# Reordering the two row-to-column boundaries of a transformer layer: tile 1's last gated residual behind tile 0's first normalised columns

## The chip, the cores and the metric

The kernel runs on one core of a Trainium2 chip. The metric is the device time of one execution in microseconds (us). The kernel before took 1943.88 us, the median of three runs (1939.19 to 1945.11).

The core has five engines that run their own instruction streams and wait for each other through semaphores: TensorE (PE in the profile, PEld for its weight loads), VectorE (DVE), ScalarE (ACT), GpSimd (POOL) and SyncE (SP, which here only issues DMAs).

## The reference

One layer over 256 tokens with 2048 features, all in float32: a SwiGLU feed-forward block, a token mixer (8 heads of softmax attention with forget gates, 4 heads of mLSTM), and a second SwiGLU block. Each block reads a modulated layernorm of the residual `x` and adds its result back through a gate, and each sum is layernormed again. Cut to what matters:

```python
ada = (silu(c) @ w_ada + b_ada)[:, None, :]
sh1, sc1, g1, sh2, sc2, g2, sh3, sc3, g3 = split(ada, 9, axis=-1)
h = swiglu(layernorm(x) * (1 + sc1) + sh1, ffn1_w_in, ffn1_w_out)
x = layernorm(ALPHA * x + 0.5 * (1 + g1) * h, ln1_g, ln1_b)
h = token_mixer(layernorm(x) * (1 + sc2) + sh2, w_in, ..., w_out)
x = layernorm(ALPHA * x + (1 + g2) * h, ln2_g, ln2_b)
h = swiglu(layernorm(x) * (1 + sc3) + sh3, ffn2_w_in, ffn2_w_out)
x = layernorm(ALPHA * x + 0.5 * (1 + g3) * h, ln3_g, ln3_b)
```

## The kernel before, in words

**Layout.** The residual `res` lies with tokens on partitions: two tiles of 128 tokens (`a` = 0 and 1), 2048 features each. The products read features on partitions: `xT` holds 16 blocks of 128 features by 256 tokens. Every float32 operand of the large products is split into a rounded part (`hi`, a cast on ACT, L142) and a rest (`lo`, a subtraction on DVE, L143), and each product is three matmuls (L367 to L369).

**A boundary.** Between a block's output product and the next block's first product the residual must be finished, normalised twice and turned from rows into columns. The function `boundary` does this, once after the first feed-forward block (the first boundary) and once after the mixer (the second one). Just ahead of it PE runs the held products of the last 512 columns, first all of tile 0, then all of tile 1. The steps, for each tile:

- `add_up`: gate times product (L431), residual (L433), statistics of the last 512 columns (L436). `row_std` then combines the statistics (L257, L259), and POOL takes the reciprocal root `rs` (L247).
- `ln_affine`: the layernorm with its gain and bias (L484, L489). ACT squares the result and sums the squares (L494).
- `ln_stats`: mean and variance of the new rows from these sums (L500 to L513). It pauses at two places: after L509, ahead of L511, which is the first step that reads ACT's sums of squares, and after POOL has been given the reciprocal root `mr` (L247), ahead of L517.
- `modulate_tile`: normalise two blocks of 128 columns (`n`: on DVE, L309, for the very first pair; on ACT, L311, for all others), transpose them on PE (`tp`, L315), scale and shift into `xf` (ACT L325, DVE L322), and split into `xhi` and `xlo` (ACT L331, DVE L332).

The first three loads of the next block's weights (`raw_mo` in the first boundary, `raw_gu` in the second) arrive early, in the three buffers that there are; the products from them (L618, `cols_1024`) read the unsplit `xf` directly, first for all of tile 0, then for all of tile 1. The fourth load waits for the buffer of the first.

**The order.** On DVE the order within a boundary is the order in which the code is written (`manual_schedule`): the function takes single steps from generators with `next`, so that the tiles' chains interleave. All other engines, and DVE elsewhere, are ordered by a scheduler from estimated durations; so a change of DVE's order in the boundary can move instructions on them too. Each engine runs its instructions in that order.

**The modulation stream.** The vector `ada` is computed beside the main products: weights of `w_ada` are streamed in (`ar`), multiplied and added on DVE (`acc`, L155 and L157), split, and summed over partitions by PE (`bc`, L170). `ada_gate` does this for a gate, in two halves of 1024 columns (`j`), each half in two parts of 512 (`i`). The gate's bias row from `b_ada` is loaded straight into `gate` by a DMA that POOL issues (L203), and L210 adds the sums to it. There is one `gate` tile: the load of the next gate's half must wait until the boundary's last L431 on these columns has read the old one. The stream is advanced a few steps at a time by `pump`; a `PAUSE` ends such a turn. `need` runs it until a given part is done.

Of the kernel before, what the change touches and what calls it, by code (L numbers as in the profile page):

```python
# [14 lines left out]
P = 128  # L15
# [17 lines left out]
def layer_kernel(  # L33
# [8 lines left out]
    V, S, G_, PE, SP = nc.vector, nc.scalar, nc.gpsimd, nc.tensor, nc.sync  # L42
# [104 lines left out]
    gate = cst.tile([P, D], F32, name="gate")  # L147
# [5 lines left out]
    def ada_acc(acc, raw, k):  # L153
        if k == 0:
            V.tensor_scalar_mul(acc, raw, csil[:, k:k + 1])  # L155
        else:
            V.scalar_tensor_tensor(out=acc, in0=raw, scalar=csil[:, k:k + 1], in1=acc,  # L157
                                   op0=ALU.mult, op1=ALU.add)


    def ada_split(acc, tag):
        ahi = ap.tile([P, 512], F32R, tag="ahi", name=f"ahi{tag}")
        alo = ap.tile([P, 512], F32R, tag="alo", name=f"alo{tag}")
        split(acc, ahi, alo)
        return ahi, alo

    def ada_sum(parts, tag):
        bc = aux_tile(f"bc{tag}")
        for i in range(2):
            PE.matmul(bc, onesr, parts[i], start=i == 0, stop=i == 1)  # L170
        return bc
# [22 lines left out]
    def ada_gate(v, s):  # L194
        for j in range(2):
            c0 = v * D + j * 1024
            acc = ap.tile([P, 1024], F32, tag="acc", name=f"acc{v}_{j}")
            for k in range(KD):
                raw = ap.tile([P, 1024], F32, tag="araw", bufs=2, name=f"ar{v}_{j}_{k}")
                SP.dma_start(raw, w_ada[0, k * P:(k + 1) * P, c0:c0 + 1024])  # L200
                ada_acc(acc, raw, k)
                yield
            G_.dma_start(gate[:, j * 1024:(j + 1) * 1024], b_ada[0:1, c0:c0 + 1024].to_broadcast([P, 1024]))  # L203
            for i in range(2):
                parts = ada_split(acc[:, i * 512:(i + 1) * 512], f"{v}_{j}_{i}")
                for _ in range(2):
                    yield PAUSE
                bc = ada_sum(parts, f"{v}_{j}_{i}")
                gs = gate[:, j * 1024 + i * 512:j * 1024 + (i + 1) * 512]
                V.scalar_tensor_tensor(out=gs, in0=bc, scalar=1.0, in1=gs, op0=ALU.add, op1=ALU.add)  # L210
                if s != 1.0:
                    V.tensor_scalar_mul(gs, gs, s)

    ada_left = {}
    PAUSE = 1
# [34 lines left out]
    def together(*gens):  # L250
        gens = list(gens)
        while gens:
            gens = [g for g in gens if next(g, 0) is None]


    def row_std(mv, rs, st):
        V.bn_aggr(mv, st)  # L257
        yield
        V.tensor_scalar_add(mv[:, 1:2], mv[:, 1:2], EPS)  # L259
        yield  # L260
        rsqrt(rs, mv[:, 1:2])
        yield

    def small(n, tag, name):
        return (wp if tag == "sums" else sm).tile([P, n], F32, tag=tag, bufs=4, name=name)
# [214 lines left out]
    def ln_affine(a, rs, mv, lgb, sums, tag):  # L480
        for h in range(2):
            cs = slice(h * (D // 2), (h + 1) * (D // 2))
            r = res[:, a, cs]
            V.scalar_tensor_tensor(out=r, in0=r, scalar=mv[:, 0:1], in1=lgb[0][:, cs],  # L484
                                   op0=ALU.subtract, op1=ALU.mult)
            yield
        for i, (c0, c1) in enumerate(((0, 1024), (1024, 1536), (1536, 2048))):
            r = res[:, a, c0:c1]
            V.scalar_tensor_tensor(out=r, in0=r, scalar=rs, in1=lgb[1][:, c0:c1], op0=ALU.mult, op1=ALU.add,  # L489
                                   accum_out=sums[:, i:i + 1])  # L490
            if i == 0:
                V.tensor_scalar_mul(sums[:, 4:5], sums[:, 0:1], -2.0 / D)
            sq = npool.tile([P, 1024], F32, tag="sq", name=f"sq_{tag}{a}{i}")
            S.activation(sq[:, :c1 - c0], r, AF.Square, bias=sums[:, 4:5], accum_out=sums[:, 7 + i:8 + i])  # L494
            yield


    def ln_stats(out_, sums):
        s = [sums[:, i:i + 1] for i in range(10)]
        V.tensor_tensor(out=s[1], in0=s[1], in1=s[2], op=ALU.add)  # L500
        yield
        mean = out_[:, 2:3]
        V.tensor_scalar(out=mean, in0=s[0], scalar1=s[1], scalar2=-1.0 / D, op0=ALU.add, op1=ALU.mult)
        yield
        V.tensor_scalar(out=s[3], in0=s[1], scalar1=s[0], scalar2=1.0 / D, op0=ALU.subtract, op1=ALU.mult)
        yield
        V.tensor_scalar(out=s[2], in0=s[3], scalar1=s[3], scalar2=-1.0, op0=ALU.mult, op1=ALU.mult)
        yield
        V.tensor_scalar_add(s[2], s[2], EPS)  # L509
        yield 1  # L510
        V.tensor_scalar(out=s[6], in0=s[7], scalar1=s[8], scalar2=s[9], op0=ALU.add, op1=ALU.add)  # L511
        yield
        V.tensor_scalar(out=s[6], in0=s[6], scalar1=1.0 / D, scalar2=s[2], op0=ALU.mult, op1=ALU.add)  # L513
        yield
        rsqrt(out_[:, 0:1], s[6])
        yield 1
        V.tensor_tensor(out=out_[:, 1:2], in0=mean, in1=out_[:, 0:1], op=ALU.mult)  # L517
        yield
# [4 lines left out]
    def boundary(add_up, st, lgb, v, tag, xT, entry, nk):  # L523
        mv, rs, sums, mr = ([small(n, t, f"{t}_{tag}{a}") for a in range(2)]
                            for n, t in ((2, "mv"), (1, "rs"), (10, "sums"), (3, "mr")))
        xs = {}
        with tc.manual_schedule(engines={mybir.EngineType.DVE}):
            for _ in add_up(0):
                pass
            together(row_std(mv[0], rs[0], st[0]))  # L530
            aff = [ln_affine(a, rs[a], mv[a], lgb, sums[a], tag) for a in range(2)]
            lns = [ln_stats(mr[a], sums[a]) for a in range(2)]
            for _ in aff[0]:
                pass
            together(lns[0])
            up = add_up(1)
            next(up)
            together(lns[0])
            m = [[modulate_tile(v, a, k, 2, mr[a], xT, xs if k < 6 else None, a + k == 0) for k in range(0, 8, 2)]
                 + [modulate_tile(v, a, k, 2, mr[a], xT) for k in range(8, nk, 2)] for a in range(2)]  # L540
            m0, m1 = m
            next(m0[0])
            together(lns[0])
            next(m0[1])
            next(up)
            next(up, 0)
            together(row_std(mv[1], rs[1], st[1]))
            next(m0[0])
            next(aff[1])
            next(m0[2])  # L550
            next(aff[1])
            next(m0[1])
            next(aff[1])
            next(m0[2])
            next(aff[1])
            next(aff[1])
            together(lns[1])
            next(m0[0])
            next(m0[1])
            together(lns[1])  # L560
            together(lns[1])
            next(m1[0])
            next(m1[1])
            next(m1[0])
            next(m1[2])
            next(m1[1])
            next(m1[2])
            for i in range(3, len(m0)):
                next(m0[i])
                next(m1[i])  # L570
                next(m0[i])
                next(m1[i])
                if i == 3:
                    for b in (m0[2], *m1[:3]):
                        next(b)
                for b in (m0[i], m1[i]):
                    next(entry, None)
                    last = next(b)
        return last, mr, xs
# [52 lines left out]
    def entry_of(load, got, u0, u1):  # L632
        for u in range(u0, u1):
            got[u] = []
            for item in load(u):
                got[u].append(item)
                yield
# [185 lines left out]
    with tc.manual_schedule(engines={mybir.EngineType.DVE, mybir.EngineType.Activation}):  # L823
        next(fa)
    ada_queue(ada_gate(2, 0.5), ada_pair(3, range(4)), ada_pair(6, range(2)), ada_gate(5, 1.0),
              ada_pair(6, range(2, 3)), ada_pair(6, range(3, 4)), ada_gate(8, 0.5))
    for j in range(4):
        fa = first_ada(j + 1) if j < 3 else load_mixer_smalls()
# [71 lines left out]
    raws = [mo_raw(u) for u in range(3)]  # L900
    mow = {}
    fence, _, xs = boundary(*ent["f"], lgb, 3, "1", xT, entry_of(mo_load, mow, 3, 6), KD)
    lnp.release()

# [456 lines left out]
    for j in range(2, 10):  # L1361
# [6 lines left out]
        for f in range(2):  # L1368
            i = 2 * j + f
# [10 lines left out]
    for j in range(2, 10):  # L1380
# [7 lines left out]
        for f in range(2):  # L1388
            i = 2 * j + f
# [51 lines left out]
```

## Time and profile before

| | |
|---|---|
| median of 3 runs | 1943.88 us (1939.19 to 1945.11) |
| the profiled execution | 1942.6 us, span of the trace 1940.9 us |
| mean granted PE clock in it | 0.994 |
| busy: PE, DVE, ACT, POOL | 1899.0, 1473.1, 945.6, 56.4 us |
| DMA | 510.90 MB, mean 263 GB/s |

The span is the time from the first to the last instruction of the profiled execution; its own time is that of the whole execution. In rows of a timeline the columns are the start in us, the duration in us, the engine, the line of the kernel, the operation, output and inputs by the names of the program, the shapes, and in brackets how long the engine stood idle before it and what ended that. In rows of stretches they are the stretch, its length, the busy time of each engine with its number of instructions, the granted PE clock (1.00 is full speed), the busy share of the DMA engines and their GB/s. In rows of a line's instructions the three numbers are the shortest, the median and the longest duration in ns.

### The profile page before, as it was taken

How to read it: one execution, taken by the hardware profiler on the slowest of the kernel's cores; microseconds unless marked ns; L12 is line 12 of the kernel's file. 1: busy time of each engine (PE TensorE's matmuls, PEld its weight loads, DVE VectorE, ACT ScalarE, POOL GpSimd, SP SyncE). 2: the span in 40 equal slices, each digit the busy share in tenths (PEclk: the TensorE clock that was granted, in tenths of full speed). 3: DMA queues.
4: the chain of work that ended last, by engine and by line, in shares of the span. 5: the costliest groups of instructions: out<-in, count | busy, mean ns of one | idle time of the engine just before them, and what ended most of it. 6: DMA issues, size and time to landing. Idle time of an engine off the chain costs nothing.

```text
span 1940.9 us, 32198 instructions
## 1 busy us (share of the span) xinstructions
PE 1899.0 (98%) x13069; PEld 1720.3 (89%) x13069; DVE 1473.1 (76%) x1818; ACT 945.6 (49%) x1336; POOL 56.4 (3%) x82
## 2 busy tenths in 40 slices
PE   6999999999999999999999999999999999999997
PEld 3999999999988888598999785998999999988886
DVE  5879988777788998688887787777766665555776
ACT  3554454443454554735755534655444444444552
POOL 1111100000000000100000000000000000000000
PEclk8999999999999999999999999999999999999999
DMA  9978869999999786499888883987776775655552
GB/s 352 382 263 313 319 229 304 305 314 311 303 321 314 273 297 210 142 312 319 266 304 289 281 295 139 315 303 243 246 255 224 269 239 196 234 185 191 194 195 87
DMA packets 295693, 510.90 MB, mean 263 GB/s; under 512 B 10834, under 2 KB 158706, under 8 KB 294520
## 3 DMA queue, kind: packets, MB, share of 16 engines
q1 hardware_dynamic: 287768, 480.53, 72.7%
q0 software_dynamic: 7776, 28.32, 4.1%
q8 instruction: 102, 1.67, 0.3%
q14 instruction: 47, 0.39, 0.1%
HBM read 506.71 MB, written 2.10 MB: 262 GB/s over the span
## 4 chain that ended last, share of the span: by engine, by line
PE 76%; issue 11%; DMA 6%; DVE 5%; ACT 1%; POOL 0%; SPq 0%; DVEq 0%; ACTq 0%; POOLq 0%
PE gu_f L369 8%; PE gu_f L367 8%; PE gu_f L368 8%; PE o_f L367 7%; PE o_f L369 7%; PE o_f L368 7%; PE s L367 4%; PE s L368 4%; PE s L369 4%; DMA ar<-in_w_ada_dram 3%; PE fh L367 2%; PE fh L369 1%; PE fh L368 1%; PE fs L367 1%; PE fs L369 1%
## 5 line engine op out<-in xcount | busy, mean ns | idle before, releaser
L157 DVE SCALAR_TENSOR_TENSOR acc<-ar,csil,acc 128x1024 f32<-128x1024 f32 x242 | 307.7, 1272 | 87.9 <-DMA ar<-in_w_ada_dram 86.7
L367 PE MATMUL s<-xhi_f,hi_s 128*128 128x256 f32 x768 | 213.2, 278 | 0.0
L368 PE MATMUL s<-xlo_f,hi_s 128*128 128x256 f32 x768 | 213.0, 277 | 0.0
L369 PE MATMUL s<-xhi_f,lo_s 128*128 128x256 f32 x768 | 212.8, 277 | 0.0
L369 PE MATMUL gu_f<-xhi_f,lo_f2i 128*128 128x256 f32 x768 | 212.0, 276 | 0.0
L367 PE MATMUL gu_f<-xhi_f,hi_f2i 128*128 128x256 f32 x768 | 212.0, 276 | 0.0
L368 PE MATMUL gu_f<-xlo_f,hi_f2i 128*128 128x256 f32 x768 | 212.0, 276 | 0.0
L143 DVE TENSOR_TENSOR lo_f2i<-raw_f2i,hi_f2i 128x1024 fp32r<-128x1024 f32 x96 | 117.5, 1224 | 87.6 <-ACT hi_f2i L142 87.5
L369 PE MATMUL gu_f<-xhi_f,lo_f1i 128*128 128x256 f32 x640 | 176.7, 276 | 0.0
L367 PE MATMUL gu_f<-xhi_f,hi_f1i 128*128 128x256 f32 x640 | 176.7, 276 | 0.0
L368 PE MATMUL gu_f<-xlo_f,hi_f1i 128*128 128x256 f32 x640 | 176.7, 276 | 0.0
L142 ACT CAST hi_f2i<-raw_f2i 128x1024 fp32r<-128x1024 f32 x96 | 100.8, 1050 | 135.2 <-PE gu_f L368 124.3
L142 ACT CAST hi_s<-raw_s 128x1024 fp32r<-128x1024 f32 x96 | 100.6, 1052 | 128.5 <-PE s L368 94.4
L368 PEld LDWEIGHTS s<-xlo_f,hi_s 128*128 128x128 f32 x768 | 144.9, 189 | 0.2 <-DVE xlo_f L299 0.2
L369 PEld LDWEIGHTS s<-xhi_f,lo_s 128*128 128x128 f32 x768 | 144.9, 189 | 0.0
L367 PEld LDWEIGHTS s<-xhi_f,hi_s 128*128 128x128 f32 x768 | 144.7, 189 | 0.0
L368 PEld LDWEIGHTS gu_f<-xlo_f,hi_f2i 128*128 128x128 f32 x768 | 144.1, 188 | 0.2
L367 PEld LDWEIGHTS gu_f<-xhi_f,hi_f2i 128*128 128x128 f32 x768 | 144.1, 188 | 0.2
L369 PEld LDWEIGHTS gu_f<-xhi_f,lo_f2i 128*128 128x128 f32 x768 | 144.1, 188 | 0.0
L143 DVE TENSOR_TENSOR lo_f2o<-raw_f2o,hi_f2o 128x1024 fp32r<-128x1024 f32 x88 | 107.7, 1224 | 44.9 <-ACT hi_f2o L142 44.8
L143 DVE TENSOR_TENSOR lo_s<-raw_s,hi_s 128x1024 fp32r<-128x1024 f32 x96 | 115.6, 1221 | 26.8 <-ACT hi_s L142 26.7
L367 PE MATMUL o_f<-hi_f2o,hh 128*128 128x512 f32 x344 | 135.2, 393 | 0.0
(485 smaller groups left out, 5351.8 us busy)
## 6 DMA issues: line engine op xcount, KB each, us to landing
ar<-in_w_ada_dram SPq DMA_DIRECT2D x227, 512.0 KB, 5.3
raw_f2i<-in_ffn_w_in_dram SPq DMA_DIRECT2D x48, 1024.0 KB, 5.1
raw_s<-in_ffn_w_in_dram SPq DMA_DIRECT2D x47, 1024.0 KB, 7.3
raw_f1o<-in_ffn_w_out_dram SPq DMA_DIRECT2D x44, 1024.0 KB, 7.2
raw_f2o<-in_ffn_w_out_dram SPq DMA_DIRECT2D x44, 1024.0 KB, 5.0
raw_f1i<-in_ffn_w_in_dram SPq DMA_DIRECT2D x40, 1024.0 KB, 7.6
ar<-in_w_ada_dram POOLq DMA_DIRECT2D x48, 512.0 KB, 6.7
raw_mxo<-in_w_out_dram SPq DMA_DIRECT2D x16, 1024.0 KB, 6.0
```

Source lines behind the costliest of these rows:

```text
L142: S.copy(hi, src)
L143: return V.tensor_tensor(out=lo, in0=src, in1=hi.bitcast(F32), op=ALU.subtract)
L157: V.scalar_tensor_tensor(out=acc, in0=raw, scalar=csil[:, k:k + 1], in1=acc, op0=ALU.mult, op1=ALU.add)
L367: PE.matmul(o, ah, bh, start=start, stop=False)
L368: PE.matmul(o, ah, bl, start=False, stop=False)
L369: PE.matmul(o, al, bh, start=False, stop=stop)
```

## The change

In `boundary`, the three steps of `add_up(1)` for tile 1's last 512 columns (gate product, residual, statistics) no longer stand at two places inside tile 0's `ln_stats`; they stand together behind the first step of tile 0's second pair of columns (`m0[1]`). In `ada_gate`, the load of the gate's bias row is written one `PAUSE` later, behind the first part's split.

```diff
@@ ada_gate
-            G_.dma_start(gate[:, j * 1024:(j + 1) * 1024], b_ada[0:1, c0:c0 + 1024].to_broadcast([P, 1024]))
             for i in range(2):
                 parts = ada_split(acc[:, i * 512:(i + 1) * 512], f"{v}_{j}_{i}")
-                for _ in range(2):
-                    yield PAUSE
+                yield PAUSE
+                if i == 0:
+                    G_.dma_start(gate[:, j * 1024:(j + 1) * 1024], b_ada[0:1, c0:c0 + 1024].to_broadcast([P, 1024]))
+                yield PAUSE
                 bc = ada_sum(parts, f"{v}_{j}_{i}")
@@ boundary
             together(lns[0])
             up = add_up(1)
-            next(up)
             together(lns[0])
...
             next(m0[0])
             together(lns[0])
             next(m0[1])
-            next(up)
-            next(up, 0)
+            for _ in up:
+                pass
             together(row_std(mv[1], rs[1], st[1]))
```

In the changed kernel the lines from L203 on stand up to four lines lower and those from L208 to the boundary one lower, so L431 of before is L432 there, and L203 is L207.

DVE in the first boundary, before; `sums_8228` and `mr_8230` are tile 0's, `o_f_7703` is tile 1's last product, `st_f_6242` and `mv_8225` tile 1's statistics:

```order
L509 TENSOR_SCALAR sums_8228<-sums_8228 128x1
L431 TENSOR_TENSOR o_f_7703<-o_f_7703,gate 128x512
L511 TENSOR_SCALAR sums_8228<-sums_8228 128x1
L513 TENSOR_SCALAR sums_8228<-sums_8228 128x1
L309 TENSOR_SCALAR n_8263<-res,mr_8230 128x256
L517 TENSOR_TENSOR mr_8230<-mr_8230 128x1
L433 SCALAR_TENSOR_TENSOR res<-res,o_f_7703 128x512
L436 BN_STATS st_f_6242<-res 128x6
```

The same place in the changed kernel:

```order
L510 TENSOR_SCALAR sums_8228<-sums_8228 128x1
L512 TENSOR_SCALAR sums_8228<-sums_8228 128x1
L514 TENSOR_SCALAR sums_8228<-sums_8228 128x1
L310 TENSOR_SCALAR n_8262<-res,mr_8230 128x256
L518 TENSOR_TENSOR mr_8230<-mr_8230 128x1
L432 TENSOR_TENSOR o_f_7703<-o_f_7703,gate 128x512
L434 SCALAR_TENSOR_TENSOR res<-res,o_f_7703 128x512
L437 BN_STATS st_f_6242<-res 128x6
```

Tile 1's gate product moved from ahead of L511 to behind L517 (now L518). The second boundary changes in the same way.

POOL at the same boundary, before, with what each instruction waits for:

```order
L247 TENSOR_TENSOR rs_8226<-mv_8224,mhalf 128x1 [waits DVE_49]
L203 DMA gate<-in_b_ada_dram 128x1024 [waits DMASW1_49,DVE_49]
L247 TENSOR_TENSOR mr_8230<-sums_8228,mhalf 128x1 [waits DVE_49]
L247 TENSOR_TENSOR rs_8227<-mv_8225,mhalf 128x1 [waits DVE_49]
L247 TENSOR_TENSOR mr_8231<-sums_8229,mhalf 128x1 [waits DVE_49]
```

And in the changed kernel:

```order
L248 TENSOR_TENSOR rs_8226<-mv_8224,mhalf 128x1 [waits DVE_49]
L248 TENSOR_TENSOR mr_8230<-sums_8228,mhalf 128x1 [waits DVE_49]
L207 DMA gate<-in_b_ada_dram 128x1024 [waits DMASW1_49,DVE_49]
L248 TENSOR_TENSOR rs_8227<-mv_8225,mhalf 128x1 [waits DVE_49]
L248 TENSOR_TENSOR mr_8231<-sums_8229,mhalf 128x1 [waits DVE_49]
```

The bias row's load moved from ahead of tile 0's `mr` to behind it. The second boundary has the same swap; the other four loads of bias rows keep their places.

PE in the first boundary where tile 0's products end and tile 1's transposes begin, before (`mo_8484` and `mo_8485` are tile 0's, `mo_8486` and `mo_8487` tile 1's; `raw_mo_8218` is the first weight load, `raw_mo_8222` the third; the first `tp` is tile 1's):

```order
L618 MATMUL mo_8484<-raw_mo_8222,xf_8297 128x512
L618 MATMUL mo_8485<-raw_mo_8222,xf_8297 128x512
L315 MATMUL tp_8322<-ident,n_8320 128x128 x2
L618 MATMUL mo_8484<-raw_mo_8222,xf_8297 128x512
L315 MATMUL tp_8327<-ident,n_8325 128x128 x2
L315 MATMUL tp_8335<-ident,n_8333 128x128 x2
L618 MATMUL mo_8485<-raw_mo_8222,xf_8297 128x512
L618 MATMUL mo_8486<-raw_mo_8218,xf_8330 128x512
```

And in the changed kernel:

```order
L618 MATMUL mo_8484<-raw_mo_8222,xf_8297 128x512
L618 MATMUL mo_8485<-raw_mo_8222,xf_8297 128x512
L618 MATMUL mo_8484<-raw_mo_8222,xf_8297 128x512
L618 MATMUL mo_8485<-raw_mo_8222,xf_8297 128x512
L316 MATMUL tp_8322<-ident,n_8320 128x128 x2
L316 MATMUL tp_8327<-ident,n_8325 128x128 x2
L618 MATMUL mo_8486<-raw_mo_8218,xf_8330 128x512
L316 MATMUL tp_8335<-ident,n_8333 128x128 x2
```

Tile 0's last two products moved ahead of tile 1's first transposes. At the second boundary one such product moves. In the mixer the scheduler also puts four steps `acc6_0` of the modulation stream (L157) one place earlier on DVE, each ahead of a split `lo_mv` of the value columns' weights.

## The prediction

> **What bounds the kernel now.** I read the page first, then the busy times in five stretches, then the timeline of each engine around the two boundaries. The page:
>
> ```profile
> span 1940.9 us, 32198 instructions
> PE 1899.0 (98%) x13069; PEld 1720.3 (89%) x13069; DVE 1473.1 (76%) x1818; ACT 945.6 (49%) x1336; POOL 56.4 (3%) x82
> ```
>
> TensorE (PE) is busy 1899.0 of 1940.9 us, so only about 42 us can be won by scheduling, wherever PE stands still. The stretches (length, then busy time of PE, PEld, DVE, ACT and POOL):
>
> ```profile
> 776.00:810.00 34.00, 30.13 (x98) 15.35 (x97) 18.25 (x44) 20.94 (x46) 3.21 (x4) 1.00 0.34 105
> 810.00:1186.00 376.00, 368.86 (x2408) 332.31 (x2407) 313.70 (x460) 202.74 (x354) 6.07 (x9) 1.00 0.86 290
> 1186.00:1217.00 31.00, 27.94 (x79) 13.84 (x79) 16.42 (x44) 18.38 (x42) 3.21 (x4) 0.94 0.24 80
> 1217.00:1930.00 713.00, 711.37 (x5055) 660.95 (x5053) 476.87 (x524) 340.70 (x438) 1.52 (x1) 1.00 0.68 226
> ```
>
> The first boundary (776 to 810) has 3.9 us without PE, the second (1186 to 1217) 3.1 us. Behind the second PE hardly stops (1.6 us in 713), so what is won there reaches the end. The mixer between them leaves 7.1 us idle. PE at the first boundary:
>
> ```profile
> 777.49 0.40 PE L369 MATMUL o_f<-hi_f1o,hl 128*128 128x512 f32 x1
> 780.69 0.41 PE L315 MATMUL tp<-ident,n 128*128 128x128 f32 x2 [2.80 <-DVE mr L517]
> 782.88 7.89 PE L618 MATMUL mo<-raw_mo,xf 128*128 128x512 f32 x18
> 791.24 0.44 PE L315 MATMUL tp<-ident,n 128*128 128x128 f32 x2 [0.46 <-ACT n L311]
> ```
>
> Its last product ends at 777.89; it then waits 2.80 us for tile 0's first normalised columns, and later 0.46 for tile 1's. The rows of VectorE (DVE), ScalarE (ACT) and GpSimd (POOL) say why:
>
> ```profile
> 766.91 0.70 DVE L431 TENSOR_TENSOR o_f<-o_f,gate 128x512 f32<-128x512 f32 x1 [5.72 <-PE o_f L369]
> 769.39 0.15 DVE L259 TENSOR_SCALAR mv<-mv 128x1 f32<-128x1 f32 x1
> ...
> 775.52 0.15 DVE L509 TENSOR_SCALAR sums<-sums 128x1 f32<-128x1 f32 x1
> 777.93 0.70 DVE L431 TENSOR_TENSOR o_f<-o_f,gate 128x512 f32<-128x512 f32 x1 [2.25 <-PE o_f L369]
> 778.53 0.27 DVE L511 TENSOR_SCALAR sums<-sums 128x1 f32<-128x1 f32 x1
> 778.83 0.21 DVE L513 TENSOR_SCALAR sums<-sums 128x1 f32<-128x1 f32 x1
> 780.13 0.41 DVE L309 TENSOR_SCALAR n<-res,mr 128x256 f32<-128x256 f32 x1 [1.08 <-POOL mr L247]
> 780.46 0.15 DVE L517 TENSOR_TENSOR mr<-mr 128x1 f32<-128x1 f32 x1
> ...
> 782.26 0.15 DVE L259 TENSOR_SCALAR mv<-mv 128x1 f32<-128x1 f32 x1
> ```
>
> ```profile
> 776.20 0.18 ACT L494 ACTIVATION_READ_ACCUMULATOR sq<-res,sums 128x1 f32 x1
> ```
>
> ```profile
> 778.93 0.58 POOL L203 DMA_DIRECT2D gate<-in_b_ada_dram  x1 [7.76 <-DVE sums L511]
> 779.52 0.57 POOL L247 TENSOR_TENSOR mr<-sums,mhalf 128x1 f32<-128x1 f32 x1
> ```
>
> ACT has tile 0's sum of squares at 776.38, but L511, which reads it, stands in DVE's order behind L431 of tile 1, and L431 waits for PE's last product. Then the reciprocal root `mr` waits once more: on POOL it stands behind the bias row's load, whose issue ends at 779.51.
>
> **The change at the first boundary.** It takes both things out of the way, and needs both: with L431 behind `mr` but the load, which waits for L431, ahead of it, the two engines would wait for each other.
>
> Tile 0: L511 can start at 776.42. From L511 to L513 is 0.30 as before; L513 takes 0.21, the root 0.57, and two hand-overs 0.04 each (780.09 to 780.13): L309 at 777.58 instead of 780.13, 2.55 us earlier. PE's transposes follow 0.56 behind L309 (780.69 against 780.13), at 778.14: PE's wait shrinks from 2.80 to 0.25.
>
> Tile 1: L431 now follows L517, at 777.58 + 0.33 + 0.07 = 777.98, only 0.05 later than before, since it had waited for PE anyway. But nothing of tile 0 stands inside its chain now. From L431 to the start of L259 is 2.48 us where the chain runs alone (766.91 to 769.39), so L259 comes at 780.46 instead of 782.26: tile 1 is 1.80 us earlier. Its order on all engines down to its first transposes is as before, so those could start at 789.44 instead of 791.24.
>
> PE between: before, it had done ten of tile 0's twelve L618 products by 790.77 (the x18 are nine of them, two records each, so about 0.86 us a product). Now ten end at 788.22, and by the new order on PE the last two come next, to 789.94. Tile 1's transposes are ready by then; PE no longer waits and stands 1.30 us earlier and two products (1.72) further, 3.0 us in all. I take 0.5 off: the two products had covered tile 1's way from transposes to features, which now runs bare (0.46 us for one such ACT step). That leaves **2.5 us**; bounds 1.3 (no use of the earlier products) and 3.0.
>
> Next in line is the fourth weight load, which needs the buffer of the first:
>
> ```profile
> 798.13 14.18 SPq L342 DMA_DIRECT2D raw_mo<-in_w_in_dram  x5
> ```
>
> It is released by PE's own tile 1 products, which move by about the same 2.5 us, so it moves along rather than becoming the bound.
>
> The load that stepped back: it is now issued once L431 ends, at about 778.7, on POOL between the two roots; tile 1's `rs` wants POOL only at 780.46 + 0.15 + 0.04 = 780.65. The issue costs 0.58, so nothing waits. All 48 loads of L746, issued from POOL beside the work of DVE, took about the same:
>
> ```profile
> L746 POOL DMA_DIRECT2D ar<-in_w_ada_dram x48: 707/722/889, 28.1 to 228.4; - x48
> ```
>
> [...]
>
> The bias row's later place otherwise costs nothing: its first reader (L210) comes a whole pause later still, and the other four such loads keep their place among POOL's rows.
>
> **The change at the second boundary.** The rows again:
>
> ```profile
> 1188.79 0.70 DVE L431 TENSOR_TENSOR o_mx<-o_mx,gate 128x512 f32<-128x512 f32 x1 [2.33 <-PE o_mx L369]
> 1190.98 0.41 DVE L309 TENSOR_SCALAR n<-res,mr 128x256 f32<-128x256 f32 x1 [1.07 <-POOL mr L247]
> 1193.12 0.15 DVE L259 TENSOR_SCALAR mv<-mv 128x1 f32<-128x1 f32 x1
> ```
>
> ```profile
> 1188.84 0.19 ACT L494 ACTIVATION_READ_ACCUMULATOR sq<-res,sums 128x1 f32 x1
> 1201.44 1.09 ACT L311 ACTIVATE n<-res,mr 128x256 f32<-128x256 f32 x2 [1.41 <-DVE mr L517]
> ```
>
> ```profile
> 1191.54 0.41 PE L315 MATMUL tp<-ident,n 128*128 128x128 f32 x2 [2.79 <-DVE mr L517]
> 1203.16 0.38 PE L315 MATMUL tp<-ident,n 128*128 128x128 f32 x2
> ```
>
> Here ACT delivers only at 1189.03, later than L431 could start. L511 starts at 1189.06, and L309 1.16 behind it as above, at 1190.22: 0.76 us earlier. L431 starts at 1190.62, and 2.48 later L259 at 1193.10: tile 1 gains nothing. PE's wait falls from 2.79 to 2.03. At 1203.16 PE itself was late for tile 1, because of its clock (stretch, PE busy, granted clock):
>
> ```profile
> 780.00:783.00 3.00, 2.05 (x9) 1.00 0.55 180
> ...
> 1193.00:1196.00 3.00, 3.00 (x6) 0.50 0.01 4
> ```
>
> After a gap of 2.79 us the clock was halved for some 3.4 us, 1.7 us of work; after the 2.80 at the first boundary it was not. If the shorter gap leaves it whole, tile 1's transposes start when ready. At the first boundary they stood 0.66 behind the start of tile 1's n:
>
> ```profile
> 790.58 1.09 ACT L311 ACTIVATE n<-res,mr 128x256 f32<-128x256 f32 x2 [1.41 <-DVE mr L517]
> ```
>
> So here they start at 1201.44 + 0.66 = 1202.10, with one product (0.86) more done: 1.06 + 0.86 - 0.5 for lost cover = 1.4. If the clock is halved again, 0.76. I take **1.3**.
>
> [...]
>
> **The sum:** 2.5 + 1.3 = 3.8 us. The profiled execution took 1942.6 (span 1940.9 and 1.7 around it), so 1938.8 for its like; it lay 1.3 below the median of 1943.88 (1939.19 to 1945.11), so **1940.1** for the median. That is 0.2% and within the 0.3%, 5.8 us, which a measurement of this kernel can about tell from no change. The bounds of the two terms, 1.3 + 0.8 to 3.0 + 1.9 (no cover lost), give 1939.0 to 1941.8.
>
> **The rivals.**
>
> *More than the sum: halved clocks go too.* A gap in the mixer was also followed by a slowed clock:
>
> ```profile
> 955.00:960.00 5.00, 5.00 (x37) 0.79 0.88 306
> ```
>
> In this stretch alone 0.21 of 5 us is lost, 1.0. If the median execution, unlike the profiled one, also has a halved clock at the first boundary, to which a gap of 0.25 gives no occasion, that adds 790.77 + 1.7 - 791.24 = 1.2; if the shifted mixer escapes its own, 1.0 more: 3.8 + 2.2 = 6.0, and, with nothing taken off for cover, 7.1: 1937.9 to 1936.8, I say 1937.4. For it: the profiled run is faster than the median. [...]
>
> *Given back in the mixer.* PE waits there for softmax steps that share DVE with the modulation stream, and that stream waits for its weights:
>
> ```profile
> 1071.00 0.33 PE L1058 MATMUL ptp<-ident,s 128*128 128x128 f32 x1 [2.39 <-ACT s L1053]
> ```
>
> If those weights come no earlier, the first boundary's 2.5 us become a longer wait here, and 1.3 remain: 1942.6. Against: their loads are issued in one queue with the products' own, so all move together.
>
> *POOL is slow.* The same root has two durations there:
>
> ```profile
> L247 POOL TENSOR_TENSOR rs<-mv,mhalf x4: 1514/1522/1534, 769.6 to 1193.4; 128x1 f32<-128x1 f32 x4
> L247 POOL TENSOR_TENSOR mr<-sums,mhalf x4: 548/561/572, 779.5 to 1200.7; 128x1 f32<-128x1 f32 x4
> ```
>
> If `mr` now takes 1.52 instead of 0.56, or the load's issue holds `rs` up by as much, tile 0 or tile 1 loses 0.96 at both boundaries: 3.8 - 1.9 = 1.9, 1942.0. Against: `rs` ran while DVE was at work, and `mr` still has a DVE that waits for it. [...]
>
> *Slower.* The changed order also puts four modulation steps (`acc6_0`, L157) one place earlier, ahead of weight splits of the value columns. Such a step waits for its weights:
>
> ```profile
> 858.85 1.28 DVE L157 SCALAR_TENSOR_TENSOR acc<-ar,csil,acc 128x1024 f32<-128x1024 f32 x1 [1.70 <-DMA ar<-in_w_ada_dram]
> ```
>
> ```profile
> 861.24 0.28 PE L368 MATMUL b_mv<-lo_mv,xhi_mx 128*128 128x256 f32 x1
> ```
>
> Behind it the third split would end at 858.85 + 1.28 + 0.69 = 860.82, and PE reads it at 861.24: 0.4 us of lead. From a load 0.4 us later on, PE stops. If each of the four costs its wait and its own length (1.70 + 1.28), that is 11.9 - 0.4 - 3.8 = 7.7 slower: 1951.6. Against: PE has no wait in that stretch before, and it needs all four late.
>
> **How the numbers follow.** Forecast 0.47; more than the sum 0.30; given back 0.10; POOL slow 0.05; slower 0.08. Faster by over 0.3% (below 1938.1) is the second case and a tenth of the first, 0.35; slower over 0.3% is the last, 0.08; within is 0.57. The range takes in the forecast, the two lesser gains and most of the larger one, with 1.3 us for the median itself: 1936.0 to 1943.9.
>
> **What would show it.** Right: PE's wait at the first L315 of the first boundary near 0.3 us and none before tile 1's first; near 2.0 at the second; `mr` ahead of the bias row on POOL, at 0.57; L259 of tile 1 some 1.8 us earlier after PE's last product at the first boundary and unmoved at the second; the raw_mo loads 2.5 us earlier against that product. Wrong: waits of PE on `lo_mv`, a `rs` that starts late behind the load, a wait longer than 2.39 at L1058, or a fourth raw_mo load that PE waits for.

## The result, and the profile after

The changed kernel took 1938.55 us in the median of 12 runs (1932.77 to 1942.37), the kernel before 1943.67 beside it (12 runs). The ratio is 0.9968 with an interval of 0.9957 to 0.9979: a gain of about 0.3%, 5.1 us between the medians, 4.1 to 8.4 by the interval. Timed once more (run `e7_again` below) it was 0.9973 [0.996, 0.9986]. One of the twelve runs of `e10_full` below took 3889.87 us and does not count in its ratio. The forecast was 1940.1, a gain of 0.2%; the measured one lies about on the 0.3% that I had set as the bound of what can be told.

The profiled execution took 1937.79 us. The page, and busy time in stretches laid at the same places as before (777.80 and 1181.30 stand where 776.00 and 1186.00 stood, counted from PE's last product of each boundary):

```profile
span 1936.1 us, 32201 instructions
PE 1895.1 (98%) x13069; PEld 1717.0 (89%) x13069; DVE 1474.7 (76%) x1818; ACT 944.7 (49%) x1336; POOL 56.4 (3%) x82
```

```profile
777.80:811.80 34.00, 33.02 (x112) 17.89 (x111) 21.07 (x48) 23.43 (x51) 3.19 (x4) 1.00 0.41 133
811.80:1181.30 369.50, 364.16 (x2394) 328.17 (x2393) 311.20 (x455) 199.86 (x349) 6.08 (x9) 1.00 0.86 293
1181.30:1212.30 31.00, 28.71 (x83) 14.13 (x82) 17.49 (x46) 18.27 (x42) 3.19 (x4) 0.94 0.24 85
1212.30:1925.30 713.00, 710.83 (x5052) 660.36 (x5050) 476.35 (x522) 340.44 (x438) 1.52 (x1) 1.00 0.67 226
```

PE's idle time fell from 3.9 to 1.0 us at the first boundary and from 3.1 to 2.3 at the second. PE at the first boundary, in the timeline of after:

```profile
779.28 0.40 PE L370 MATMUL o_f<-hi_f1o,hl 128*128 128x512 f32 x1
779.86 0.44 PE L316 MATMUL tp<-ident,n 128*128 128x128 f32 x2 [0.19 <-DVE n L310]
782.15 9.61 PE L618 MATMUL mo<-raw_mo,xf 128*128 128x512 f32 x22
791.59 0.60 PE L316 MATMUL tp<-ident,n 128*128 128x128 f32 x4
792.52 1.12 PE L618 MATMUL mo<-raw_mo,xf 128*128 128x512 f32 x2 [0.33 <-ACT xf L326]
804.02 0.80 PE L368 MATMUL mo<-hi_mo,xhi_mx 128*128 128x512 f32 x1
```

The wait ahead of tile 0's transposes is 0.19 us instead of 2.80, and tile 1's first transposes (791.59) wait for nothing. The last row is the first product with split weights; from the start of PE's last product (the first row) to its start is 24.74 us. I call this the boundary's stretch; in the kernel before it was 27.44. DVE and POOL at the same place:

```profile
777.31 0.15 DVE L510 TENSOR_SCALAR sums<-sums 128x1 f32<-128x1 f32 x1
778.20 0.27 DVE L512 TENSOR_SCALAR sums<-sums 128x1 f32<-128x1 f32 x1 [0.74 <-ACT sq L495]
779.39 0.41 DVE L310 TENSOR_SCALAR n<-res,mr 128x256 f32<-128x256 f32 x1 [0.67 <-POOL mr L248]
779.79 0.69 DVE L432 TENSOR_TENSOR o_f<-o_f,gate 128x512 f32<-128x512 f32 x1
782.26 0.15 DVE L260 TENSOR_SCALAR mv<-mv 128x1 f32<-128x1 f32 x1
```

```profile
778.81 0.54 POOL L248 TENSOR_TENSOR mr<-sums,mhalf 128x1 f32<-128x1 f32 x1 [5.86 <-DVE sums L514]
780.78 0.57 POOL L207 DMA_DIRECT2D gate<-in_b_ada_dram  x1 [1.42 <-DVE o_f L432]
782.50 1.53 POOL L248 TENSOR_TENSOR rs<-mv,mhalf 128x1 f32<-128x1 f32 x1 [1.15 <-DVE mv L260]
```

DVE now waits only for ACT's sums and for the root, and the gate product stands behind. The second boundary, with rows of DVE, ACT and PE:

```profile
1179.26 0.15 DVE L493 TENSOR_SCALAR sums<-sums 128x1 f32<-128x1 f32 x1
1184.37 0.27 DVE L512 TENSOR_SCALAR sums<-sums 128x1 f32<-128x1 f32 x1 [2.60 <-ACT sq L495]
1185.55 0.41 DVE L310 TENSOR_SCALAR n<-res,mr 128x256 f32<-128x256 f32 x1 [0.66 <-POOL mr L248]
1188.43 0.15 DVE L260 TENSOR_SCALAR mv<-mv 128x1 f32<-128x1 f32 x1
```

```profile
1181.39 1.15 ACT L495 ACTIVATE sq<-res,sums 128x1024 f32<-128x1024 f32 x1 [12.37 <-DVE sums L506]
```

```profile
1183.66 0.40 PE L370 MATMUL o_mx<-hi_mxo,ylo 128*128 128x512 f32 x1
1186.02 0.44 PE L316 MATMUL tp<-ident,n 128*128 128x128 f32 x2 [1.96 <-DVE n L310]
1198.59 0.60 PE L316 MATMUL tp<-ident,n 128*128 128x128 f32 x4
1210.63 0.80 PE L368 MATMUL ge<-hi_gu,xhi_f 128*128 128x512 f32 x1
```

Here DVE waits 2.60 us for ACT's squares, and PE 1.96 us for DVE. ACT starts the first square at 1181.39, though the bias that it reads (L493) was there at 1179.41. That gap of 2.0 us is what the experiments from the third on are about.

### The profile page after: what moved, and what is told of

Read it like the earlier page. It is cut to its first block, busy times and chain, and to the rows that moved or that the text cites. A ratio compares the mean times of both kernels' runs of the same rounds, so it can differ in the third digit from the quotient of the medians.

```text
span 1936.1 us, 32201 instructions
## 1 busy us (share of the span) xinstructions
PE 1895.1 (98%) x13069; PEld 1717.0 (89%) x13069; DVE 1474.7 (76%) x1818; ACT 944.7 (49%) x1336; POOL 56.4 (3%) x82
## 4 chain that ended last, share of the span: by engine, by line
PE 75%; issue 11%; DMA 6%; DVE 5%; ACT 2%; POOL 0%; SPq 0%; DVEq 0%; ACTq 0%; POOLq 0%
PE gu_f L369 8%; PE gu_f L370 8%; PE gu_f L368 8%; PE o_f L368 7%; PE o_f L370 7%; PE o_f L369 7%; PE s L369 5%; PE s L368 5%; PE s L370 5%; DMA ar<-in_w_ada_dram 3%; PE fh L368 2%; PE fh L370 2%; PE fh L369 1%; PE fs L370 1%; PE fs L369 1%
## 5 line engine op out<-in xcount | busy, mean ns | idle before, releaser
L157 DVE SCALAR_TENSOR_TENSOR acc<-ar,csil,acc 128x1024 f32<-128x1024 f32 x242 | 307.8, 1272 | 84.4 <-DMA ar<-in_w_ada_dram 83.2
```

## The experiments

The question is which of three things moved the time: the order at either boundary, the bias row, or the clock; and what holds the second boundary. Each kernel was timed beside the kernel before.

**One boundary at a time, and the bias row alone.** `e1_first` and `e2_second` are the changed kernel with the old order kept at the other boundary:

```
             up = add_up(1)
+            if not tag == "1":      # e2_second: "2"
+                next(up)
             together(lns[0])
```

> The new order at the first boundary only; the second is as before. Theory (gain by shorter waits of PE at the boundaries, 2.7 us at the first and 0.7 at the second, and a shorter stall in the mixer that follows the first): 2.7 to 6 us faster than before. If the changed order in the mixer is what brings the extra 3 us seen in the trace of the changed kernel, it is in this run too, and the stretch from the first boundary's last product to the second's is again near 404 us (before 411). Rival (the extra is chance of one execution): about 2.7 us faster and a stretch near 408. In either case the second boundary's wait of PE for tile 0's columns is back at 2.8 us.

> The new order at the second boundary only. Theory: 0.7 us faster than before, too little to be told from none by the times; in the trace PE waits 2.0 us there instead of 2.8, and the first boundary's 2.8 us are as before. The mixer's order is word for word that of before, so the stretch between the boundaries' last products is near 411 us if order and start decide it, and may be anything from 404 to 411 if chance does.

`e3_row` is the kernel before with the new place of the bias row's load alone (the first part of the diff). Without the new order the scheduler leaves the load ahead of `mr`, so the order on every engine is that of before, and the run cannot show what the load's place behind `mr` is worth inside the change. By the rows of before, `mr` could have started at 779.08, 0.04 us behind the end of L513, instead of 779.52: an estimate of 0.44 us.

> The bias row's load a pause later and nothing else. The order on every engine is that of before, also on POOL, where the load still stands ahead of mr. Both theories: same time, ratio 1.000 within its interval; it shows what two kernels with one order differ by, and its trace is a second look at the waits of before. Rival (the later load is worth something by itself, by less traffic or an earlier mr): 0.4 us or more at each boundary, mr starting less than 0.1 us behind L513's end.

Measured against the kernel before: the first boundary alone 0.9988 [0.9974, 1.0001], the second alone 1.0003 [0.9989, 1.0017], the row alone 1.0002 [0.9991, 1.0013]. These intervals overlap and each holds 1, so the times alone do not tell the two boundaries apart, nor do the two ratios add up to the 0.9968 of both, which stays open. The traces say how much each gives, in the table below. PE waits 0.18 us at the first boundary and 2.79 at the second in `e1_first`, and 2.79 and 1.96 in `e2_second`: each boundary's wait follows its own order. From the last product of the first boundary to that of the second it is 407.9 us in `e1_first`, against 410.9 before and 404.4 after, so the 404 did not come back, as its rival had it; `e2_second` has 412.6, more than expected either way. `e2_second` and `e3_row` have the order of before at the first boundary, and there the clock of PE dropped, which it had not in the profile before. The 6 us that begin 3 us behind PE's last product, in before, `e2_second` and `e3_row`:

```profile
780.50:786.50 6.00, 5.55 (x17) 2.75 (x18) 5.86 (x12) 4.35 (x12) 1.51 (x1) 1.00 0.24 78
```

```profile
781.60:787.60 6.00, 5.78 (x11) 2.75 (x12) 5.86 (x12) 4.54 (x12) 1.51 (x1) 0.50 0.25 83
```

```profile
781.90:787.90 6.00, 5.54 (x13) 2.58 (x14) 5.86 (x12) 4.44 (x12) 1.51 (x1) 0.72 0.23 83
```

The granted clock (third number from the end) was 1.00, 0.50 and 0.72, with 17, 11 and 13 matmuls done, after gaps of 2.79 to 2.80 us.

**Where ACT's squares wait.** In the changed kernel the scratch for the squares (`sq`, L494) is a tile of a pool that takes over memory released by the mixer. `e5_squares` lays it in another part of that pool, meant to overlap nothing that PE still reads:

```
         ent["np"] = tc.alloc_tile_pool(name="np3", bufs=1, **right)
+        ent["np"].tile([P, 1024], F32, tag="sq", name="sq_place")
+        gap(ent["np"], 4608, "gap_sq")
```

> The changed kernel with the scratch tile of the squares moved by 4608 bytes at the second boundary, order on every engine unchanged. Theory: in the second boundary ACT's first square waited for PE, because its scratch tile lies where the last readers of head 0's mixer output are still being multiplied: it started 2.0 us behind the sums it needs, where at the first boundary it started 0.12 behind them. Moved, it starts 0.1 to 0.2 us behind them, tile 0's columns come 2 us earlier, PE waits about 0.2 us instead of 2.0, tile 1 comes 1.8 us earlier, and the time is 2 to 2.5 us below the changed kernel's, 7 to 8.5 below before. Rival (ACT is held by something else, such as a function table or its queue): no change against the changed kernel.

It failed: the square still began 2.0 us late, and PE still waited 1.96 us. The time was 0.9982 [0.997, 0.9994], no better than the changed kernel.

```profile
1186.40 0.15 DVE L493 TENSOR_SCALAR sums<-sums 128x1 f32<-128x1 f32 x1
```

```profile
1188.54 1.15 ACT L495 ACTIVATE sq<-res,sums 128x1024 f32<-128x1024 f32 x1 [11.58 <-DVE sums L506]
```

The rows of PE tell what the square waits for. The tiles `yh` and `yl` lie in the released pool, `yhi` and `ylo`, which PE reads next, do not. The last products that read `yl`, in after and in `e5_squares`:

```profile
1180.92 0.39 PE L370 MATMUL o_mx<-hi_mxo,yl 128*128 128x512 f32 x1
```

```profile
1188.06 0.39 PE L370 MATMUL o_mx<-hi_mxo,yl 128*128 128x512 f32 x1
```

In both the square starts 0.08 to 0.09 us behind the end of this product. So moving the tile within the pool changed nothing. That the wait is for the last reader of any tile in the pool, wherever the new tile lies, fits this, but no run varies the place further. What is left to try is to leave that pool. `e6_scratch` is the changed kernel with it in the pool of the norm's parameters:

```
-    gap(lnp, 224, "gap_y")
+    gap(lnp, 96, "gap_y")
...
-            sq = npool.tile([P, 1024], F32, tag="sq", name=f"sq_{tag}{a}{i}")
+            sq = (lnp.tile([P, 1024], mybir.dt.bfloat16, tag="sq", name=f"sq_{tag}{a}{i}") if tag + str(a) == "20"
+                  else npool.tile([P, 1024], F32, tag="sq", name=f"sq_{tag}{a}{i}"))
```

> The changed kernel, with the scratch of tile 0's three squares at the second boundary laid in the pool that holds the norm's parameters instead of the pool that is taken from the mixer's released memory (as bfloat16, since nothing reads it; the order of DVE, POOL and SP is word for word that of the changed kernel). Theory: at the second boundary the squares' wait for PE's last reader of the whole released pool is what leaves the change only 0.8 us there. Then ACT's first square starts 0.1 to 0.3 us behind its sums instead of 2.0, tile 0's first normalised columns come some 2 us earlier, PE waits 0.2 to 0.5 us instead of 2.0 between its last product and tile 0's transposes, the clock stays whole behind them, and from PE's last product to the first high product of the next sublayer it is 24.9 to 25.2 us instead of 25.9 to 27.0. Median 1.5 to 2.5 us below the changed kernel in the same call. Rival: the second boundary is bound by tile 1's chain or by the weights' splits; then the stretch stays above 25.8 us and the time within 0.5 us.

`e9_oldscratch` makes the same edit in the kernel before, whose order it keeps:

> The kernel before, in its old order word for word, with the scratch of the second boundary's three squares of tile 0 moved as in e6. Theory: the old order's own DVE work (tile 1's last gate product, residual and statistics ahead of tile 0's first columns) ends as late as the squares' wait, so that either hides the other: the first square starts 2 us earlier, but PE still waits 2.3 to 2.8 us, and the time stays within 0.6 us of the kernel before. The two then are worth more together than apart. Rival: the two add; then PE waits 0.8 us here and the time falls by some 2 us without any change of order.

And the changed kernel ran with them again:

> The changed kernel once more, beside the others of this call: 0.996 to 0.998 of the kernel before. PE waits 0.2 us at the first boundary, with a whole clock behind it; it waits 2.0 us at the second, where the clock may be halved or not. If the first boundary shows a halved clock, the clock is not a matter of the wait there.

`e6_scratch` took 1936.23 us, 0.9956 [0.9942, 0.997]; `e7_again` 1940.23, 0.9973 [0.996, 0.9986]; the kernel before 1946.64 beside them. So `e6_scratch` is the fastest version, 4.0 us below the changed kernel by the medians and 3.3 by the ratios. The intervals of the ratios overlap, but the means of the two sets of 12 runs differ by 3.3 us with a 95% interval of 0.8 to 5.9. Its rows at the second boundary, ACT and then PE (the edit moves L495 of the changed kernel to L496):

```profile
1185.84 1.15 ACT L496 ACTIVATE sq<-res,sums 128x1024 bf16<-128x1024 f32 x1 [9.68 <-DVE sums L493]
```

```profile
1190.09 0.40 PE L370 MATMUL o_mx<-hi_mxo,ylo 128*128 128x512 f32 x1
1190.47 0.44 PE L316 MATMUL tp<-ident,n 128*128 128x128 f32 x2
1213.99 0.79 PE L368 MATMUL ge<-hi_gu,xhi_f 128*128 128x512 f32 x1
```

The square starts as soon as its sums are there, and takes the same 1.15 us with its bfloat16 output as with float32. PE goes from its last product to the transposes with no wait, and the stretch is 23.90 us instead of 26.96 in `e7_again`. That is more than expected: 24.9 to 25.2 us of stretch and 1.5 to 2.5 us of time had been said.

In `e9_oldscratch` the squares come as early, and nothing is won: 1.0001 [0.9987, 1.0014]. The old order holds DVE behind the gate product, for just as long (ACT, DVE, PE; the edit moves L494 of before to L495):

```profile
1184.85 1.15 ACT L495 ACTIVATE sq<-res,sums 128x1024 bf16<-128x1024 f32 x1 [9.69 <-DVE sums L492]
```

```profile
1189.54 0.70 DVE L431 TENSOR_TENSOR o_mx<-o_mx,gate 128x512 f32<-128x512 f32 x1 [2.38 <-PE o_mx L369]
1191.74 0.41 DVE L309 TENSOR_SCALAR n<-res,mr 128x256 f32<-128x256 f32 x1 [1.08 <-POOL mr L247]
```

```profile
1192.30 0.41 PE L315 MATMUL tp<-ident,n 128*128 128x128 f32 x2 [2.80 <-DVE mr L518]
```

Two things delayed tile 0 at the second boundary, side by side. Taking away the order alone gives 0.7 us, the squares' wait alone nothing, both 3.8 (27.70 to 23.90, 1.0 of it clock).

**The clock by itself.** `e8_filled` and `e10_full` are the kernel before with useless matmuls in the gaps, 11 and 22 of them; `e11_second_full` is the changed kernel with 15 at the second boundary. All else stands in its place.

```
+            fill = aux_tile(f"fill_{tag}")
+            for _ in range(11):      # e10_full: 22; e11_second_full: 15, at tag "2" alone
+                PE.transpose(fill[:, :P], res[:, 0, :P], ident)
             together(lns[0])
             up = add_up(1)
```

> The kernel before, with 11 matmuls 128x128 of no use (transposes of columns long done, into a tile that nobody reads) put on PE between the last product and tile 0's first transposes at both boundaries; every other instruction stands as before. It keeps PE busy in the gaps of 2.8 us and changes no wait of the other engines. Theory: the gap is what halves the clock. Then the granted clock behind both gaps is 1.00, the first boundary's stretch is 27.4 us (its value with a whole clock) rather than up to 29.6, the second's 26.5 to 27.0 instead of 27.7, and the median is 1 to 2.5 us below the kernel before: the part of the change's gain that is clock. Rival: the clock falls there for another reason (load ahead of the gap); then it is 0.50 to 0.72 behind one or both gaps and the time stays within 0.5 us.

> The kernel before with 22 useless matmuls on PE at each boundary instead of the 11 of e8, which took 1.36 us and left a gap of 1.60 us; 22 take 2.7 us, so PE is left idle for 0.1 to 0.4 us. Theory: the idle time is what lowers the clock behind the boundaries. Then the granted clock is 1.00 behind both, the stretch from the last product to the next high product is 27.3 to 27.5 us at the first boundary and 26.4 to 26.8 at the second (27.7 with the gap), and the median falls by 0.7 to 1.5 us (0.9992 to 0.9996 and less of the kernel before): the clock's own part of the change. Rival: the clock falls there by itself; then the second boundary stays at 27.6 to 27.7 us with 0.72.

> The changed kernel with 15 useless matmuls on PE at the second boundary alone, 1.86 us in its gap of 1.96. Theory: with PE busy there the clock is 1.00 behind the boundary, and the stretch is 25.9 to 26.0 us (the value of the run with the whole clock there) instead of 26.97; the median 0 to 1 us below the changed kernel. Rival: 0.72 in spite of it and 26.9 us.

I had sized the fill of `e8_filled` from the transposes' rows, at some 0.22 us each; it took 0.12, so a gap of 1.60 us stayed. That was enough for the clock to fall at the second boundary, though not at the first, and the time was 1.0002 [0.9988, 1.0016] instead of 1 to 2.5 us less. PE, and the 6 us behind:

```profile
1194.49 1.36 PE L537 MATMUL fill<-ident,res 128*128 128x128 f32 x11
1197.45 0.41 PE L315 MATMUL tp<-ident,n 128*128 128x128 f32 x2 [1.60 <-DVE mr L517]
```

```profile
1197.30:1203.30 6.00, 5.59 (x13) 2.72 (x14) 5.86 (x12) 4.49 (x12) 1.51 (x1) 0.72 0.21 84
```

In `e10_full` hardly a gap is left, tile 0's transposes stand where they stood, and the clock is whole:

```profile
1190.19 2.56 PE L537 MATMUL fill<-ident,res 128*128 128x128 f32 x22
1193.14 0.41 PE L315 MATMUL tp<-ident,n 128*128 128x128 f32 x2 [0.39 <-DVE mr L517]
```

```profile
1193.00:1199.00 6.00, 5.59 (x17) 2.75 (x18) 5.86 (x11) 4.40 (x12) 1.51 (x1) 1.00 0.22 79
```

All traces together, with PE's wait ahead of tile 0's transposes, the granted clock in the 6 us, and the stretch; figures in us but for the clock:

| run | first: order, wait, clock, stretch | second: order, wait, clock, stretch |
|---|---|---|
| before | old, 2.80, 1.00, 27.44 | old, 2.79, 0.72, 27.70 |
| e3_row | old, 2.80, 0.72, 28.45 | old, 2.80, 0.72, 27.55 |
| e9_oldscratch | old, 2.80, 0.72, 28.07 | old, 2.80, 0.72, 27.72 |
| e8_filled | old, 1.60, 1.00, 27.44 | old, 1.60, 0.72, 27.54 |
| e10_full | old, 0.40, 1.00, 27.44 | old, 0.39, 1.00, 26.69 |
| e2_second | old, 2.79, 0.50, 29.56 | new, 1.96, 0.72, 26.88 |
| e1_first | new, 0.18, 1.00, 24.74 | old, 2.79, 0.72, 27.69 |
| after | new, 0.19, 1.00, 24.74 | new, 1.96, 0.72, 26.97 |
| e7_again | new, 0.19, 1.00, 24.74 | new, 1.96, 0.72, 26.96 |
| e5_squares | new, 0.18, 1.00, 24.74 | new, 1.96, 1.00, 25.92 |
| e11_second_full | new, 0.19, 1.00, 24.74 | new, 0.33, 1.00, 25.92 |
| e6_scratch | new, 0.19, 1.00, 24.76 | new and squares, 0, 1.00, 23.90 |

Where PE waited 1.6 us or more the clock fell in 11 of 14 boundaries, where it waited 0.4 or less in none of 10. So in these traces a gap made the fall likely, and its length alone did not decide it. A fallen clock costs 0.8 to 1.1 us at the second boundary (27.54 to 27.72 against 26.69, 26.88 to 26.97 against 25.92) and 0.6 to 2.1 at the first. In the time of the whole kernel a single microsecond of this kind could not be seen: `e10_full` was 1.0004 [0.999, 1.0019], which neither shows nor excludes the 0.7 to 1.5 us expected of it, and `e11_second_full` 0.9981 [0.9969, 0.9992], no lower than the changed kernel's 0.9968 and 0.9973.

## Why the prediction was right

**The first boundary, 2.5 us (1.3 to 3.0).** It measured 2.70 with a whole clock on both sides. Step by step, counted from PE's last product: L309 came 2.53 us earlier (2.55 said), PE's wait fell to 0.19 (0.25), tile 1's L259 came 1.79 earlier (1.80), its transposes 1.44 earlier (1.30) and with two more products ahead of them. The cover that those two had given cost one step of ACT, 0.33 us in the row at 792.52, where I had taken off 0.5. In all PE waited 3.5 us in this boundary before (2.80, and 0.7 for later columns) and 0.8 after (0.2, 0.3 for tile 0's second pair of columns and this 0.3): that difference is the 2.70. The fourth weight load moved along, as said, from 20.64 us behind the last product to 17.81:

```profile
797.09 13.85 SPq L343 DMA_DIRECT2D raw_mo<-in_w_in_dram  x5
```

**The bias row.** On POOL `mr` stands ahead of it and takes 0.54 us while DVE waits for it (0.57 before, also with DVE idle); the load's issue took 0.57 beside a DVE at work, and `rs` started 0.09 us behind its input, with 1.15 us of idle POOL ahead of it. So the rival of a slow POOL did not come true. In the traces of before and after no issue of a bias row took over 0.591 us.

**The second boundary, 1.3 us.** The mechanism was right and the size was off. L309 came 0.74 us earlier (0.76 said), L259 not at all (4.77 behind the last product before and after), PE's wait fell to 1.96 (2.03). But of my two ends I took the one with a whole clock, 1.4, nearly in full, and the clock was lowered again in the trace of after: 0.73 of stretch, near the other end, 0.76. That a shorter gap would leave it whole was the weak step: it did in one of four traces with a gap of 1.96 us. Where it did (`e5_squares`, 25.92) the boundary had won 1.78 on before, more than the 1.4 said. With a whole clock on both sides (26.69 in `e10_full`) the order gives 0.77. In the profiled pair the two boundaries together gave 3.4 us of the 3.8 said.

**The clock.** The length of a gap alone does not decide: gaps of 2.79 to 2.80 us were followed by a clock of 1.00, 0.72 and 0.50, gaps of 1.96 us by 0.72 three times and 1.00 once, and gaps of 1.60 us by 1.00 at the first boundary and 0.72 at the second. What else decides is not shown.

**The rival "more than the sum".** It was partly true, and may be why the median fell by more than the 3.8 said. The profile before happened to have a whole clock at the first boundary; three more traces with that order and that gap did not. The mean of these four stretches is 28.38 us. If the timed runs are like them, the new order, at 24.74 to 24.76 in six traces, is worth 3.6 there and not 2.7. With 0.73 at the second boundary that is 4.4 us, an estimate from few executions, inside both intervals (4.1 to 8.4, and 2.7 to 7.8 from `e7_again`). The rest of the 5.1 is not explained and may be chance.

The other half of that rival, a mixer that escapes its own lowered clock, came true in the profiled execution, but not by the order. Where before has 0.79, `e1_first`, which has the new order at the first boundary, has 0.79 too, while after has 1.00 (`e1_first`, then after):

```profile
954.00:959.00 5.00, 5.00 (x37) 5.00 (x37) 4.72 (x12) 5.00 (x11) 0.00 (x0) 0.79 0.61 200
```

```profile
954.00:959.00 5.00, 5.00 (x39) 4.75 (x38) 5.00 (x13) 4.97 (x7) 0.00 (x0) 1.00 0.70 207
```

Of the twelve traces two of the six with the old order at the first boundary have the clock lowered there, and two of the six with the new one.

**Given back, or slower, in the mixer.** Neither shows in the profiled execution. Its trace lists what PE waited for in the mixer (line, releaser; sum, times, longest); no `lo_mv` is among the lines, and the wait at L1058 is shorter than the 2.39 before:

```profile
PE ptp L1058 <- ACT s L1053: 1.9, 2, 1.7
PE ptp L1058 <- DVE gate L211: 1.6, 1, 1.6
```

But `e7_again`, the same kernel, shows the mechanism of "slower" once. The fourth of the moved modulation steps waits 1.80 us for its weights, the split behind it comes late, and PE waits for that:

```profile
863.25 1.28 DVE L157 SCALAR_TENSOR_TENSOR acc<-ar,csil,acc 128x1024 f32<-128x1024 f32 x1 [1.80 <-DMA ar<-in_w_ada_dram]
```

```profile
865.20 0.38 PE L369 MATMUL b_mv<-lo_mv,xhi_mx 128*128 128x256 f32 x1 [1.67 <-DVE lo_mv L143]
```

The other five traces of the new order have no wait on `lo_mv`; those of the old order have none over 0.4 us. So this rival named a real cost, of 1.7 us in one execution of six, and not the 11.9 of all four steps.

The 4.8 us by which the profiled spans differ must not be read as 2.7 + 0.7 and 1.4 more from the change. The mixer, from the first product with split weights to the last product of the second boundary, is 3.8 us shorter in after than in before (379.6 against 383.4; some 1.7 of that is the clock in before, 0.87 and 0.79 in the two stretches of 5 us from 950 to 960), and the stretches ahead of the first and behind the second boundary give 2.4 of it back. But the same order gave a mixer of 387.4 us in `e5_squares`:

```profile
803.44 0.80 PE L368 MATMUL mo<-hi_mo,xhi_mx 128*128 128x512 f32 x1
...
1190.81 0.40 PE L370 MATMUL o_mx<-hi_mxo,ylo 128*128 128x512 f32 x1
```

Over six traces each, mixers of the old order average 384.1 us and of the new one 383.5, with a spread of 4 and 8 us within each. So the 3.8 is one execution's chance, and on average the new order there costs nothing that can be seen.

## What to carry to other kernels

Where an engine runs in program order, look for the step that waits for the last event and stands ahead of work that is ready: moving it back costs its own chain nothing if that chain waited for the same event anyway. Two delays that run side by side must both go before either pays in full: here one was an order and the other a scratch buffer in reused memory, worth 0.7 and 0 us alone and 3.8 together, 1.0 of it clock. To price a change of 0.2% compare a stretch between two fixed events over several traces, for the difference of two spans carries the chance of all other parts.

## What the runs showed that was not expected

- A tile in memory taken from a released pool made ACT wait 2.0 us, until PE's last product from a tile of that pool had ended, and a move within the pool did not change it (`e5_squares`). The profile named the last step of DVE as what ended that wait; only the start of the square, 2.0 us behind its sums and 0.08 behind that product, gave the real one away, and with the tile in another pool the wait was gone (`e6_scratch`).
- A gap of PE as short as 1.60 us was followed by a granted clock of 0.72 over the next 6 us, at 0.85 us of stretch (27.54 against 26.69); with matmuls of no use in the gap it was 1.00 in `e10_full` and `e11_second_full`.
- Back-to-back transposes of 128x128 took 0.12 us each (22 in 2.56 us), while a pair behind a wait shows as 0.41 to 0.44.
